# One head per stationary in the SSD layer's diagonal product: [high | low] of one head against its own decay matrix

## The chip, the cores and the metric

The kernel runs on one core of a Trainium2 chip. The metric is the device time of one execution in microseconds (us), the median of three runs before the change. The profile is of one further execution, whose span and time stand in the table below.

## The reference, cut to what matters

One layer of a decoder trunk is computed for 256 positions of width 2048: a Mamba-2 SSD mixer, then a cross-attention into 256 memory tokens, then a gated ConvFFN, each between two RMS norms, all in fp32. The change lies in the SSD mixer, in the part within a chunk (two chunks of 128 positions, 64 heads of 64 channels, 8 groups with common B and C):

```python
a = dt * (-jnp.exp(a_log))
a_cs = cumsum(a)                       # per head, along the positions of a chunk
xdt = xs * dt[..., None]
decay = exp(where(causal, a_cs[l] - a_cs[s], -inf))
cb = einsum('bclgn,bcsgn->bgcls', cm, bm)
y_diag = einsum('bgjcls,bcsgjp->bclgjp', cb[:, :, None] * decay, xdt)
...
y = y_diag + y_off + xs * d_skip
y = rmsnorm(y * silu(z), norm_g) ; return y @ w_out
```

The kernel does not carry the states from one chunk to the next separately. It treats the 256 positions as one causal product: for each head a decay matrix M of three 128x128 blocks (source chunk 0 to target chunk 0, source 0 to target 1, source 1 to target 1), and y = M applied to xdt.

## The kernel before, in words

All activations are held transposed: channels on the 128 partitions, 256 positions along the free axis. Each weight matrix comes from memory in chunks of 128x2048 fp32 (one DMA of 1 MB each on SyncE's queue) into `raw` (3 buffers), and every half chunk is split into a high part in fp32r (`hi`, ScalarE, line 139) and the remainder (`lo`, VectorE, line 153). `hi` and `lo` have 5 buffers each. An fp32 product is then made of fp32r products: `mm3` (lines 242 to 244) adds high*high, high*low and low*high; `mm2` (lines 248 and 249) does the same with a moving operand of 512 columns [high | low] for the high weights and one of 256 for the low weights.

The work is a list of slots, one for each block of 128 output channels. A slot of the SSD projections has 16 x 3 matmuls of 256 columns (line 242 to 244, `pj<-H`). The slots go by group of heads: C, B, and then four times x and z, where one x block (index i, 32 of them) holds two heads of 64 channels. Between the matmuls of the projections hang the steps of the SSD product, as hooks of later slots. For block i they are:

- `decay` and `decay_exp` (ScalarE): the exponents of the decay matrices, four blocks at a time.
- `mk_m(i)`: decay times cb on VectorE (line 515), then its high and low parts `Mh` (ScalarE, line 262) and `Ml` (VectorE, line 264), 128x768 each, one buffer each. The columns are ordered by block, then head, then target position: (a=3, h=2, l=128).
- `xs_tr(i)` and `xdt(i)`: x transposed by TensorE, multiplied by dt on VectorE into the tile `xd` (line 542, one buffer), and its high and low parts in `xdr` (ScalarE line 262, VectorE line 264).
- `y_mm(i)`: six matmuls into one PSUM bank `py` (one buffer). The stationary holds both heads' 64 channels, so each head's M is multiplied with both heads' channels: 512 columns for source chunk 0 (three matmuls), 256 for source chunk 1 (three matmuls). On rows 0 to 63 the columns of head 0 are used, on rows 64 to 127 those of head 1.
- `y_post(i)`: on VectorE, for each head, x times d_skip plus y (line 576), then times silu(z) (line 578), then the high and low parts into `G` (ScalarE line 266, VectorE line 268), the square (ScalarE line 581) and its sum (VectorE line 290).

`G` holds 16 blocks; after blocks 0 to 15 the first half of the output projection runs (16 slots with `mm2`), and after blocks 16 to 31 the second half. The order of each engine's instructions is not written out for this part: the Tile framework's scheduler merges the steps in an order of its own by a simulated time line. Each engine then takes its instructions in that order, and waits for semaphores where data or buffers are not ready.

Of the kernel before, what the change touches and what calls it, by code (L numbers as in the profile page):

```python
# [7 lines left out]
F32 = mybir.dt.float32  # L8
FR = mybir.dt.float32r
I32 = mybir.dt.int32  # L10
AF = mybir.ActivationFunctionType
OP = mybir.AluOpType

T = 256
# [13 lines left out]
PV = {}  # L28
# [33 lines left out]
def hybrid_layer_kernel(ctx, tc, xT, memT, pvd, alog, w_dt, w_in, w_kv, w_q, w_out, w_o, w_up, w_dn, out):  # L62
    nc = tc.nc
    V, S, P, PE = nc.vector, nc.scalar, nc.gpsimd, nc.tensor
# [8 lines left out]
    pv = consts.tile([128, PVN], F32, name="pv")  # L73
# [12 lines left out]
    def col(name, j):  # L86
        return pv[:, PV[name] + j:PV[name] + j + 1]
# [4 lines left out]
    B = {}  # L92
# [127 lines left out]
    def new_chunk(src, n, kind="w"):  # L220
        chunks.append((src, n, kind))
        return len(chunks) - 1
# [18 lines left out]
    def mm3(ps, whi, wlo, xhi, xlo, start, stop):  # L241
        PE.matmul(ps, whi, xhi, start=start, stop=False)  # L242
        PE.matmul(ps, whi, xlo, start=False, stop=False)  # L243
        B["mm"] = PE.matmul(ps, wlo, xhi, start=False, stop=stop)  # L244
# [13 lines left out]
    def hilo(dst, src, scale=None):  # L258

        hi, lo = dst  # L260
        if scale is None:
            S.activation(hi, src, AF.Copy)  # L262
            yield
            return V.tensor_tensor(lo, src, hi.bitcast(F32), op=OP.subtract)  # L264
        else:
            S.activation(hi, src, AF.Copy, scale=scale)
            yield
            return V.scalar_tensor_tensor(lo, src, scale, hi.bitcast(F32), op0=OP.mult, op1=OP.subtract)
# [5 lines left out]
    def halves(t):  # L274
        return t[:, 0:T], t[:, T:2 * T]
# [71 lines left out]
    wA = phA.enter_context(tc.tile_pool(name="wA", bufs=1))  # L347
# [190 lines left out]
    def xdt(i):  # L538
        def fn():
            ps = B.pop(("pt", i))  # L540
            f = wA.tile([128, T], F32, name="xd", bufs=1)
            V.tensor_tensor(f.rearrange("p (a h c) -> p a h c", a=2, h=2),
                            ps[:, :T].rearrange("p (a h c) -> p a h c", a=2, h=2),
                            dtt[:, :, 2 * i:2 * i + 2, None].to_broadcast([128, 2, 2, 64]), op=OP.mult)
            d = wA.tile([128, 2 * T], FR, name="xdr", bufs=1)
            yield from hilo(halves(d), f)
            B["xd", i] = d
        return fn

    def y_mm(i):  # L550
        def fn():
            mh, ml = B.pop(("M", i))
            d = B.pop(("xd", i))
            ps = psum.tile([128, 512], F32, name="py", bufs=1)
            mm3(ps[:, :], d[:, 0:128], d[:, 256:384], mh[:, 0:512], ml[:, 0:512], True, False)
            mm3(ps[:, 256:512], d[:, 128:256], d[:, 384:512], mh[:, 512:768], ml[:, 512:768], False, True)
            B["y", i] = ps
        return fn

# [6 lines left out]

    def y_post(i):
        def fn():
            y = B.pop(("y", i)).rearrange("p (a h l) -> p a h l", a=2, h=2)
            x = B.pop(("xsT", i)).rearrange("p (a l) -> p a l", a=2)  # L570
            sz = B.pop(("sz", i))
            t = wA.tile([128, T], F32, name="yt", bufs=1)
            t3 = t.rearrange("p (a l) -> p a l", a=2)
            for h in range(2):
                q = slice(64 * h, 64 * h + 64)
                V.scalar_tensor_tensor(t3[q], x[q], pv[q, PV["dsk"] + i:PV["dsk"] + i + 1], y[q, :, h],
                                       op0=OP.mult, op1=OP.add)
            V.tensor_tensor(t, t, sz, op=OP.mult)
            yield from hilo(halves(G[:, i % GS]), t, col("ng", i))
            sq = wA.tile([128, T], F32, name="sqy", bufs=2)  # L580
            S.activation(sq, t, AF.Square)
            yield
            ssd_norm.add(sq)
        return fn
# [44 lines left out]
    for kind, i in order:  # L629
# [13 lines left out]
        elif kind == "x":  # L643
            lane(s, w_in[blk_no], 2048, movH, xs_post(i))
            blk_no += 1
            d = 2 if i < 2 else 0
# [252 lines left out]
    for j in range(KD):  # L899
        if j % 4 == 0:  # L900
            c = new_chunk(w_o[j // 4], 2048)
# [155 lines left out]
    for i, s in enumerate(slots):  # L1057
# [29 lines left out]
        for k in range(nk):  # L1087
            for ln, ps in zip(lanes, pss):
# [4 lines left out]
                c, off, mov = ln[0], ln[1], ln[2]  # L1093
# [4 lines left out]
                x = mov[k]  # L1098
# [123 lines left out]
```

## Time and profile before

| | |
|---|---|
| median of 3 runs | 1561.46 us (1561.24 to 1563.09) |
| the profiled execution's own time | 1564.64 us |
| its span, first to last instruction | 1562.8 us |
| mean granted TensorE clock | 0.996 of 2.4 GHz |
| busy share of the span | PE 99%, weight loads 91%, DVE 77%, ACT 62%, POOL 1% |
| matmuls, weight loads | 10316, 10316 |

PE is TensorE, PEld its weight loads, DVE VectorE, ACT ScalarE, POOL GpSimd, SP SyncE. Busy times are the union of an engine's instructions. Matmuls are pipelined, so that a matmul's duration is longer than the interval to the next one's start; it is the interval that the engine's time is made of. The same holds to a smaller degree for DVE and ACT. Lines are those of the kernel before.

### The profile page before, as it was taken

The page shows a single profiled execution, that of the slowest core. Times are in us where ns is not written, and L with a number is a line of the kernel's source. Part 1 is how long each engine was busy: PE and PEld are TensorE (multiplying, and loading weights), DVE is VectorE, ACT ScalarE, POOL GpSimd, SP SyncE. Part 2 cuts the span into 40 slices and gives each one's busy share as a digit, 9 for nine tenths or more (in the row PEclk, how much of TensorE's full clock was granted, in tenths as well). Part 3 has the DMA queues.
Part 4 walks back from the last instruction along what each step waited for, and adds up shares of the span by engine and source line. Part 5 has one row for each costly group of instructions (what it writes and reads, how often), then busy time and mean ns, then how long its engine had stood idle before and what let it go on. Part 6 is the DMA issues. An engine that isn't in the chain of part 4 may idle for free. (4 is left out here: it accounts for less than half of the span.)

```text
span 1562.8 us, 25940 instructions
## 1 busy us (share of the span) xinstructions
PE 1540.4 (99%) x10316; PEld 1415.5 (91%) x10316; DVE 1202.6 (77%) x1917; ACT 966.0 (62%) x1576; POOL 10.4 (1%) x16
## 2 busy tenths in 40 slices
PE   8999999999999999999989999999999999999998
PEld 7999999889999999888989888888888888888886
DVE  7799989655898987969777887655877766778774
ACT  6698887644777774856565655544555533555563
POOL 0000000000000000000000000000000000000000
PEclk9999999999999999999989999999999999999999
DMA  7665555555555554855444555555555555555462
GB/s 268 219 217 189 174 201 189 195 189 188 160 201 178 178 170 143 314 190 169 156 137 153 196 189 187 179 200 189 189 192 188 183 198 188 192 191 193 155 212 78
DMA packets 47289, 292.10 MB, mean 187 GB/s; under 512 B 5504, under 2 KB 5568, under 8 KB 19776
## 3 DMA queue, kind: packets, MB, share of 16 engines
q1 hardware_dynamic: 46448, 289.34, 54.1%
q8 instruction: 81, 1.33, 0.4%
q10 hardware_dynamic: 720, 1.11, 0.2%
q14 instruction: 40, 0.33, 0.1%
HBM read 288.26 MB, written 2.16 MB: 186 GB/s over the span
## 5 line engine op out<-in xcount | busy, mean ns | idle before, releaser
L139 ACT ACTIVATE hi<-raw 128x1024 fp32r<-128x1024 f32 (+2 forms) x518 | 539.9, 1045 | 485.9 <-PE pj L248 386.0
L153 DVE TENSOR_TENSOR lo<-raw,hi 128x1024 fp32r<-128x1024 f32 (+2 forms) x518 | 624.1, 1207 | 262.4 <-ACT hi L139 258.0
L248 PE MATMUL pj<-H,hi 128*128 128x512 f32 x1472 | 511.8, 392 | 1.1 <-DVE ev L910 1.1
L248 PE MATMUL pj<-G,hi 128*128 128x512 f32 x1202 | 417.1, 392 | 0.0
L249 PE MATMUL pj<-H,lo 128*128 128x256 f32 x1472 | 411.6, 280 | 0.0
L242 PE MATMUL pj<-H,hi 128*128 128x256 f32 x1280 | 361.5, 283 | 6.7 <-ACT hi L262 6.3
L244 PE MATMUL pj<-H,lo 128*128 128x256 f32 x1280 | 360.2, 282 | 0.8 <-DVE lo L264 0.7
L243 PE MATMUL pj<-H,hi 128*128 128x256 f32 x1280 | 360.3, 282 | 0.0
L249 PE MATMUL pj<-G,lo 128*128 128x256 f32 x1202 | 335.4, 280 | 0.0
L248 PEld LDWEIGHTS pj<-H,hi 128*128 128x128 f32 x1472 | 276.4, 188 | 61.6 <-ACT hi L139 1.3
L249 PEld LDWEIGHTS pj<-H,lo 128*128 128x128 f32 x1472 | 276.4, 188 | 0.0
L248 PEld LDWEIGHTS pj<-G,hi 128*128 128x128 f32 x1202 | 225.3, 188 | 49.2
L242 PEld LDWEIGHTS pj<-H,hi 128*128 128x128 f32 x1280 | 241.5, 189 | 8.9 <-ACT hi L262 7.5
L244 PEld LDWEIGHTS pj<-H,lo 128*128 128x128 f32 x1280 | 241.9, 189 | 2.1 <-DVE lo L264 1.6
L243 PEld LDWEIGHTS pj<-H,hi 128*128 128x128 f32 x1280 | 242.0, 189 | 1.0
L249 PEld LDWEIGHTS pj<-G,lo 128*128 128x128 f32 x1202 | 225.7, 188 | 0.4
L920 DVE SCALAR_TENSOR_TENSOR fu<-ev,pv,fu 128x255 f32<-128x255 f32 (+1 forms) x176 | 84.2, 480 | 2.8
L456 DVE SCALAR_TENSOR_TENSOR u<-ev,pv,u 128x255 f32<-128x255 f32 (+2 forms) x144 | 68.5, 478 | 5.1 <-ACT u L452 3.9
L916 ACT ACTIVATE fu<-ev,pv 128x256 f32<-128x256 f32 x88 | 51.7, 589 | 1.4 <-DVE ev L913 0.9
L367 DVE TENSOR_TENSOR ev<-pj,rx 128x256 f32<-128x256 f32 x80 | 33.6, 421 | 13.2 <-PE pj L244 10.4
L255 DVE TENSOR_TENSOR ev<-pj,ev 128x256 f32<-128x256 f32 x92 | 38.4, 417 | 0.0
L262 ACT ACTIVATE Mh<-dec 128x768 fp32r<-128x768 f32 x32 | 26.9, 841 | 16.4 <-PE py L244 15.6
(270 smaller groups left out, 1400.8 us busy)
## 6 DMA issues: line engine op xcount, KB each, us to landing
raw<-in_w_up_dram SPq DMA_DIRECT2D x88, 1024.0 KB, 4.8
raw<-in_w_in_dram SPq DMA_DIRECT2D x78, 1024.0 KB, 4.9
raw<-in_w_out_dram SPq DMA_DIRECT2D x32, 1024.0 KB, 4.9
raw<-in_w_dn_dram SPq DMA_DIRECT2D x32, 960.0 KB, 4.6
raw<-in_w_dn_dram SPq DMA_DIRECT2D x16, 896.0 KB, 4.5
rows<-rows_d SPq DMA_DIRECT2D x32, 256.0 KB, 3.7
raw<-in_w_kv_dram SPq DMA_DIRECT2D x8, 1024.0 KB, 4.8
raw<-in_w_q_dram SPq DMA_DIRECT2D x4, 1024.0 KB, 4.8
```

The source lines that it names most:

```text
L139: S.activation(hi_t[c, h][:, :b - a], raw_t[c][:, a:b], AF.Copy)
L153: V.tensor_tensor(lo_t[c, h][:, :b - a], raw_t[c][:, a:b], hi_t[c, h][:, :b - a].bitcast(F32), op=OP.subtract)
L242: PE.matmul(ps, whi, xhi, start=start, stop=False)
L243: PE.matmul(ps, whi, xlo, start=False, stop=False)
L244: B["mm"] = PE.matmul(ps, wlo, xhi, start=False, stop=stop)
L248: PE.matmul(ps, whi, x, start=start, stop=False)
L249: B["mm"] = PE.matmul(ps[:, T:], wlo, x[:, 0:T], start=False, stop=stop)
L255: V.tensor_tensor(t, ps[:, :T], t, op=OP.add)
L367: V.tensor_tensor(t, ps[:, :T], x_norm.rbc, op=OP.mult)
L456: V.scalar_tensor_tensor(u[:, d:], ps[:, :T - d], pv[:, w + j:w + j + 1], u[:, d:], op0=OP.mult, op1=OP.add)
L916: S.activation(u, t, AF.Identity, bias=col("fb", blk), scale=pv[:, w + 2:w + 3])
L920: V.scalar_tensor_tensor(u[:, d:], t[:, :T - d], pv[:, w + j:w + j + 1], u[:, d:], op0=OP.mult, op1=OP.add)
```

## The change

In `xdt`, the high and low parts of the two heads are laid out as [high 0 | low 0 | low 1 | high 1] for each source chunk, in a tile of 128 x 768 with gaps. In `y_mm`, each head has a stationary of its own, its 64 high and its 64 low channels; the moving operand is that head's part of `Mh`, then of `Ml`: 256 columns for source chunk 0 (two pieces of 128), 128 columns for source chunk 1. That is eight matmuls, four of 256 and four of 128 columns. The result of head 0 has its high part on rows 0 to 63 and its low part on rows 64 to 127; for head 1 it is the other way round. In `y_post`, two ScalarE copies bring the low rows to the other 64 partitions, into a tile `u` that takes the buffer of `xd`, and VectorE adds them.

```diff
@@ xdt
-            d = wA.tile([128, 2 * T], FR, name="xdr", bufs=1)
-            yield from hilo(halves(d), f)
-            B["xd", i] = d
+            d = wA.tile([128, 2, 2, 192], FR, name="xdr", bufs=1)
+            flat = d.rearrange("p a h x -> p a (h x)")
+            lo = flat[:, :, 64:192].rearrange("p a (h c) -> p a h c", h=2)
+            yield from hilo((d[:, :, :, 0:64], lo), f.rearrange("p (a h c) -> p a h c", a=2, h=2))
+            B["xd", i] = flat
@@ y_mm
-            mm3(ps[:, :], d[:, 0:128], d[:, 256:384], mh[:, 0:512], ml[:, 0:512], True, False)
-            mm3(ps[:, 256:512], d[:, 128:256], d[:, 384:512], mh[:, 512:768], ml[:, 512:768], False, True)
+            m4 = [x.rearrange("p (a h l) -> p a h l", a=3, h=2) for x in (mh, ml)]
+            for h in range(2):
+                o = ps[:, h * T:(h + 1) * T]
+                for k, x in enumerate(m4):
+                    PE.matmul(o.rearrange("p (a l) -> p a l", a=2), d[:, 0, 128 * h:128 * h + 128], x[:, 0:2, h],
+                              start=k == 0, stop=False)
+                for k, x in enumerate(m4):
+                    PE.matmul(o[:, 128:], d[:, 1, 128 * h:128 * h + 128], x[:, 2, h], start=False, stop=k == 1)
@@ y_post
-            y = B.pop(("y", i)).rearrange("p (a h l) -> p a h l", a=2, h=2)
-            x = B.pop(("xsT", i)).rearrange("p (a l) -> p a l", a=2)
+            y = B.pop(("y", i)).rearrange("p (h l) -> p h l", h=2)
+            x = B.pop(("xsT", i))
             sz = B.pop(("sz", i))
+            u = wA.tile([128, T], F32, name="xd", bufs=1)
+            S.activation(u[0:64], y[64:128, 0], AF.Copy)
+            S.activation(u[64:128], y[0:64, 1], AF.Copy)
             t = wA.tile([128, T], F32, name="yt", bufs=1)
-            t3 = t.rearrange("p (a l) -> p a l", a=2)
             for h in range(2):
                 q = slice(64 * h, 64 * h + 64)
-                V.scalar_tensor_tensor(t3[q], x[q], pv[q, PV["dsk"] + i:PV["dsk"] + i + 1], y[q, :, h],
+                V.scalar_tensor_tensor(t[q], x[q], pv[q, PV["dsk"] + i:PV["dsk"] + i + 1], y[q, h],
                                        op0=OP.mult, op1=OP.add)
+            V.tensor_tensor(t, t, u, op=OP.add)
             V.tensor_tensor(t, t, sz, op=OP.mult)
```

## Rows read from the trace of the kernel before

**Rows 1.** The page: busy time by engine, and the 40 slices in tenths.
```profile
PE 1540.4 (99%) x10316; PEld 1415.5 (91%) x10316; DVE 1202.6 (77%) x1917; ACT 966.0 (62%) x1576; POOL 10.4 (1%) x16
PE   8999999999999999999989999999999999999998
```
**Rows 2.** Windows of both SSD halves: stretch, its length, busy us (instructions) by engine.
```profile
80.00:283.00 203.00, 203.00 (x1669) 200.57 (x1668) 183.97 (x305) 170.35 (x302) 0.00 (x0) 1.00 0.56 191
365.00:610.00 245.00, 245.00 (x2015) 241.98 (x2014) 207.95 (x333) 172.11 (x290) 0.00 (x0) 1.00 0.53 179
```
**Rows 3.** Waits, 80 to 283 us: engine, line, releaser: total us, times, longest.
```profile
ACT hi L139 <- PE pj L243: 17.1, 21, 2.3
ACT Mh L262 <- PE py L244: 5.3, 5, 1.5
...
DVE lo L153 <- ACT hi L139: 2.2, 6, 0.5
```
**Rows 4.** Waits, 365 to 610 us.
```profile
ACT hi L139 <- PE pj L243: 42.9, 38, 2.1
DVE lo L153 <- ACT hi L139: 22.6, 30, 3.4
...
ACT hi L139 <- PE pj L248: 6.5, 4, 1.7
```
**Rows 5.** Groups by line and shape on PE: busy us, mean ns of one.
```profile
L242 PE MATMUL py<-Mh,xdr 128*128 128x512 f32 x32 | 12.6, 394 | 0.0
...
L242 PE MATMUL py<-Mh,xdr 128*128 128x256 f32 x32 | 9.0, 280 | 0.0
```
**Rows 6.** Time line of PE, a y product: start us, duration us, instruction.
```profile
193.75 0.39 PE L244 MATMUL py<-Mh,xdr 128*128 128x512 f32 x1
193.98 0.28 PE L242 MATMUL py<-Mh,xdr 128*128 128x256 f32 x1
194.10 0.28 PE L243 MATMUL py<-Ml,xdr 128*128 128x256 f32 x1
194.21 0.28 PE L244 MATMUL py<-Mh,xdr 128*128 128x256 f32 x1
194.33 0.28 PE L243 MATMUL pj<-H,hi 128*128 128x256 f32 x1
```
**Rows 7.** Time line of PE, cb product with three matmuls of 128 columns.
```profile
62.26 0.22 PE L242 MATMUL ms<-CT,BT 128*128 128x128 f32 x1
62.32 0.28 PE L243 MATMUL ms<-CT,BT 128*128 128x128 f32 x1
62.43 0.27 PE L244 MATMUL ms<-CT,BT 128*128 128x128 f32 x1
62.54 0.33 PE L243 MATMUL pj<-H,hi 128*128 128x256 f32 x1
62.72 0.28 PE L244 MATMUL pj<-H,lo 128*128 128x256 f32 x1
```
**Rows 8.** Time line of the weight loads in the same place.
```profile
62.27 0.19 PEld L243 LDWEIGHTS ms<-CT,BT 128*128 128x128 f32 x1
62.37 0.19 PEld L244 LDWEIGHTS ms<-CT,BT 128*128 128x128 f32 x1
62.48 0.19 PEld L243 LDWEIGHTS pj<-H,hi 128*128 128x128 f32 x1
```
**Rows 9.** Time line of DVE, a y_post and the next block's xd.
```profile
195.37 0.97 DVE L576 SCALAR_TENSOR_TENSOR yt<-xsT,pv,py 64x256 f32<-64x256 f32 x2
...
198.12 0.42 DVE L578 TENSOR_TENSOR yt<-yt,sz 128x256 f32<-128x256 f32 x1
198.46 1.22 DVE L153 TENSOR_TENSOR lo<-raw,hi 128x1024 fp32r<-128x1024 f32 x1
...
200.04 0.41 DVE L542 TENSOR_TENSOR xd<-pt,dtt 128x256 f32<-128x256 f32 x1
```
**Rows 10.** Time line of ACT, a copy out of PSUM and the instruction behind it.
```profile
291.41 0.37 ACT L607 ACTIVATE m<-pj 128x256 f32<-128x256 f32 x1
291.67 1.05 ACT L139 ACTIVATE hi<-raw 128x1024 fp32r<-128x1024 f32 x1
```
**Rows 11.** Time line of DVE, the last block's G.
```profile
618.75 0.48 DVE L268 SCALAR_TENSOR_TENSOR G<-yt,pv,G 128x256 fp32r<-128x256 f32 x1 [0.58 <-ACT G L266]
```
**Rows 12.** Time line of PE, second output projection behind it.
```profile
622.66 0.62 PE L248 MATMUL pj<-G,hi 128*128 128x512 f32 x2
```

## The prediction, made before the result was known

> **What bounds the kernel now.** I read the page first, then the windows of the stage that the change touches, then who waits there, and last the time lines around single instructions. The page has TensorE (PE) busy 99% of the span, with only the first, one midway and the last of the 40 slices below nine tenths [rows 1]. The SSD product lies in two stretches, blocks 0 to 15 at about 80 to 283 us and blocks 16 to 31 at about 365 to 610 us. In both PE is busy for every microsecond: 203.00 of 203.00 and 245.00 of 245.00 [rows 2]. So in this stage the time is the number of PE's instructions times their intervals, and an interval taken from PE is time won, unless another engine comes to pace it. The nearest is VectorE (DVE): 183.97 of 203.00 busy in the first half (idle 19.0 us), 207.95 of 245.00 in the second (idle 37.1 us). ScalarE (ACT) idles for 32.7 and 72.9 us [rows 2]. What ACT waits for is mostly a free buffer for the next split (hi waits for pj: 17.1 us in 21 waits in the first half, 42.9 and 6.5 us in the second) [rows 3, 4]. A split that waits for a buffer is as far ahead as it can be, so this is time that ACT can give away. The first half has less than half of it.
>
> **PE, the term that decides.** A matmul's duration (394 ns for 512 columns, 280 ns for 256) [rows 5] is not what it takes of PE, since the next one starts earlier. The intervals: the 512-column y matmul starts at 193.75 and the next at 193.98, so 0.23 us; the three of 256 columns run from 193.98 to 194.33, so 0.117 us each [rows 6]. A block before takes 3 x 0.23 + 3 x 0.117 = 1.04 us of PE.
>
> After, a block takes eight matmuls, four of 256 and four of 128 columns. Columns fall by a third, from 2304 to 1536. But the page counts as many weight loads as matmuls [rows 1], so two matmuls with the same stationary still load it twice, and the eight have eight loads. What a 128-column fp32r matmul takes is seen in the cb product: three of them start at 62.26, the projection's matmul behind them at 62.54 and the one behind that at 62.72 [rows 7]. From 62.26 to 62.72 there are three of 128 and one of 256 columns: (0.46 - 0.117) / 3 = 0.114 us each. The weight loads there start 0.10 and 0.11 us apart [rows 8]: at 128 columns the load of the next weights sets the interval, not the columns. A 128-column matmul thus takes nearly what a 256-column one does. New block: 4 x 0.117 + 4 x 0.114 = 0.92 us. Gain 0.12 us, over 32 blocks 3.8 us.
>
> The bounds: one interval in that place is 0.06 us (62.26 to 62.32) [rows 7]. At 0.06 for all four, a block is 0.71 us and the gain 10.6 us. I take 0.114, because the short interval is repaid behind it (0.18 us from 62.54 to 62.72). On the other side, the 256-column operand is now two pieces of 128 with a gap, which no row shows. At worst it costs two intervals of 128 columns, 0.228 us, which is 0.44 us a block or 14.2 us more, a loss of 10.4 us in all; at best 0.105 us, the interval of the loads [rows 8], 1.5 us more gain. I take 0.117, the contiguous row of the same number of elements.
>
> The Trainium skill, in "TensorE: Matmul & The Clock Gate", section "Back-to-back issue gap", gives about 81 ns for each matmul of 128 columns in a sustained stream of loads and matmuls. By that figure a block would be 4 x 0.117 + 4 x 0.081 = 0.79 us and the gain 8.0 us, by estimate. The trace here has 114 ns in its own such stream, so it speaks against that figure.
>
> **DVE and ACT, the terms that should be hidden.** For each block y_post gains one DVE add of 128x256 in SBUF. Its nearest row is the multiplication on the line behind it: 0.42 us long, the next instruction 0.34 us after its start [rows 9]. 32 x 0.34 = 10.9 us on DVE, 5.4 us in each half. The two scalar_tensor_tensors keep 64x256 and read contiguous instead of strided columns; I take 0 for that: the two take 0.97 us now [rows 9], at best they would take two of the add's intervals, 0.68 us (0.3 us a block less on DVE), and nothing in their shape has grown. The high and low parts of xdr keep their element counts and get gaps, also 0. ACT gains two copies of 64x256 out of PSUM; the row is a copy of 128x256 out of PSUM, with the next instruction 0.26 us after its start [rows 10]. That is 0.52 us a block, 16.6 us in all, 8.3 us in each half. The other partition half as the target is not seen before; between 0.26 and twice that for each copy I take 0.26, since the columns set it. The cover is the idle time in rows 2: 5.4 us into 19.0 on DVE, 8.3 us into 32.7 on ACT in the first half. If the cover were gone, the 5.4 us would reach PE there.
>
> **New waits.** The copies wait at the head of ACT's queue for the last y matmul, and behind them stand the splits and Mh of the next block. ACT waits for that same event already, for Mh: 5 times, 5.3 us in the first half [rows 3]. The add waits for the copies. The tile u shares xd's one buffer, so the next block's xd multiplication (L542) waits for the add, with splits queued behind it on DVE. In the trace L576 starts at 195.37, the next L542 at 200.04 [rows 9]: 4.7 us, in which 0.97 us of L576 and the add fit. u itself waits for xd's last reader, which comes ahead of the y matmuls anyway. No DMA is added or moved on SP's queue. At the end of the stage the last block's G is written by 618.75 + 0.48 us [rows 11] and first read at 622.66 us [rows 12] (before that stand 45 matmuls of three output blocks that read the other 15): 3.4 us, against at most 0.52 + 0.34 us and the hand-over in between. All at 0.
>
> **The sum.** The profiled execution is 1564.64 us, its span 1562.8 us. 1564.64 - 3.8 = 1560.8 us. The runs' median lies 3.2 us below that execution, so the forecast for the median is 1561.46 - 3.8 = 1557.7 us. About 0.2%, 3.1 us, can be told from no change: below 1558.3 us is faster, above 1564.6 us slower. The forecast is just beyond that edge.
>
> **Rivals.**
> 1. DVE takes the first half. It is busy 91% there, and the scheduler merges everything anew. For: ACT and DVE hand splits to each other in that half with little waiting for buffers. Against: 19.0 us are idle, and PE did not wait once. If half of the added 5.4 us reaches PE, 1557.7 + 2.7 = 1560.4 us; if all, 1563.1 us. No change.
> 2. The copies block ACT's queue (the slower side). If each copy pair waits like Mh does, 5.3 / 5 = 1.06 us, a block costs ACT 1.06 + 0.52 = 1.58 us, in the first half 16 x 1.58 = 25.3 us, against 17.1 us of waits for buffers that can give way. 8.2 us then reach PE: 1557.7 + 8.2 = 1565.9 us. It decides from a wait of 17.1 / 16 - 0.52 = 0.55 us a block on. In the second half 25.3 us stay below 42.9 + 6.5 us. Against: the list of waits has 5 such waits for 16 blocks, so the scheduler mostly places what follows y late enough. The gapped operand at its upper bound (1561.46 + 10.4 = 1571.9 us) goes with this side.
> 3. The weight loads don't pace the 128-column matmuls: 1561.46 - 10.6 = 1550.9 us. For: the one short interval. Against: the sum of four intervals behind it.
> 4. The change does nothing, because PE would not be the bound: excluded by rows 2.
>
> **How the numbers follow.** Forecast 0.52, within 1556 to 1560 us, of which 0.36 lies below 1558.3 us and 0.16 above. Rival 1: 0.21, nearly all of it no change. Rival 2 with the gapped operand: 0.15. Rival 3: 0.12. Faster 0.36 + 0.12 = 0.48; same 0.16 + 0.20 = 0.36; slower 0.01 + 0.15 = 0.16. The range takes in the forecast, rival 1 and the nearer parts of 2 and 3: 1552.5 to 1565 us.
>
> **What would show it.** In the changed kernel's time line, a y matmul of 128 columns takes 0.11 us to the next start in the mean (right) or 0.06 (rival 3); a block's eight matmuls take 0.92 us together. The page counts 10316 + 64 matmuls and as many loads. PE stays busy in every microsecond of the SSD halves; idle time with DVE lo L153 or ACT hi L139 as the releaser means rival 1 or 2, and the waits of the copies for py tell which. DVE's busy time there grows by about 32 x 0.42 us, ACT's by 64 x 0.37. The forecast is wrong if the gapped operand's interval is above 0.13 us, or if PE idles for more than 1 us between 40 and 610 us.

## The result: 1578.9 us, slower

The changed kernel takes 1578.86 us (median of 4 runs, 1578.39 to 1580.44) against 1562.07 us of the kernel before in the same series, a ratio of 1.0106 with a 95% interval of 1.0095 to 1.0118. That is 16.8 us slower, where 3.8 us faster was forecast. The profiled execution took 1580.44 us, its span is 1578.7 us, 15.9 us more than before.

The page of the changed kernel, its busy times, the 40 slices of PE and the granted clock:

```profile
PE 1545.5 (98%) x10380; PEld 1422.5 (90%) x10380; DVE 1214.0 (77%) x1949; ACT 992.2 (63%) x1640; POOL 10.4 (1%) x16
PE   8999999799999999999989999999999999999998
...
PEclk9999999899999999999999999999999999999999
```

There is one new hole in PE, in the eighth slice, where before every slice but three was full [rows 1], and the clock falls in the same slice. The windows of the changed kernel around it (stretch, length, busy us and instructions of PE, PEld, DVE, ACT and POOL, granted clock, DMA share, GB/s):

```profile
100.00:280.00 180.00, 180.00 (x1509) 179.55 (x1508) 162.16 (x272) 149.27 (x270) 0.00 (x0) 1.00 0.54 183
280.00:300.00 20.00, 18.15 (x112) 16.05 (x110) 14.15 (x25) 11.17 (x24) 0.00 (x0) 1.00 0.46 163
300.00:320.00 20.00, 10.29 (x35) 8.13 (x36) 12.98 (x25) 17.27 (x34) 0.00 (x0) 0.66 0.11 25
320.00:340.00 20.00, 20.00 (x107) 17.47 (x107) 11.23 (x13) 9.19 (x13) 0.00 (x0) 0.91 0.70 238
400.00:640.00 240.00, 240.00 (x1993) 237.99 (x1992) 205.17 (x338) 179.52 (x313) 0.00 (x0) 1.00 0.53 176
```

Inside the SSD stretches PE is as full as before [rows 2]: 180.00 of 180.00 and 240.00 of 240.00 us. The loss lies between the first half and the second, in the first output projection. PE's time line there:

```profile
297.87 0.27 PE L565 MATMUL py<-Ml,xdr 128*128 128x128 f32 x1
303.08 0.80 PE L248 MATMUL pj<-G,hi 128*128 128x512 f32 x1 [4.93 <-DVE G L268]
303.68 0.41 PE L249 MATMUL pj<-G,lo 128*128 128x256 f32 x1
303.89 0.63 PE L248 MATMUL pj<-G,hi 128*128 128x512 f32 x1
304.31 0.41 PE L249 MATMUL pj<-G,lo 128*128 128x256 f32 x1
...
307.80 0.36 PE L562 MATMUL py<-Mh,xdr 128*128 128x256 f32 x1 [1.79 <-DVE xdr L264]
```

The output projection waits for the G of block 14 (4.93 us), then block 15's product waits for its `xdr` (1.79 us), and so on: 11.56 us of marked waits between 280 and 340 us (4.93, 1.79, 0.82, 3.14 and 0.88). After the first of them the interval of a 512-column matmul is 0.42 us (303.89 to 304.31) instead of 0.23 [rows 6]: the granted clock has dropped to its lower level, 1.2 GHz. It stands there from 303.1 to 306.5 us and again from 309.9 to 323.5 us. The longer intervals add 7.2 us (each interval from 270 to 345 us less its mean at the upper level and less the marked waits). 11.6 + 7.2 = 18.8 us lost. Against that stands what the product gains, below.

### The profile page after: what moved, and what is told of

The parts are those of the page before. It is cut to its first block, busy times and chain, and to the rows that moved or that the text cites. A ratio compares the mean times of both kernels' runs of the same rounds, so it can differ in the third digit from the quotient of the medians.

```text
span 1578.7 us, 26223 instructions
## 1 busy us (share of the span) xinstructions
PE 1545.5 (98%) x10380; PEld 1422.5 (90%) x10380; DVE 1214.0 (77%) x1949; ACT 992.2 (63%) x1640; POOL 10.4 (1%) x16
## 5 line engine op out<-in xcount | busy, mean ns | idle before, releaser
L248 PE MATMUL pj<-G,hi 128*128 128x512 f32 x1202 | 422.5, 395 | 9.6 <-DVE G L268 8.3
L264 DVE TENSOR_TENSOR Ml<-dec,Mh 128x768 fp32r<-128x768 f32 x32 | 30.6, 955 | 11.3 <-ACT Mh L262 10.6
```

Of the source, the lines that this page charges most:

```text
L248: PE.matmul(ps, whi, x, start=start, stop=False)
```

## Why block 15 is late: the start's lag, and a loop that can't make it up

Counted in the time lines, block 0's product starts at 86 us in both kernels, after 12.3 slots of the projections (their matmuls counted, 48 to a slot). The hooks ask for it after 6. The stage thus begins six slots late, and before the change the blocks made that up: block 12 starts 1.3 slots behind its hook (36.4 against 35.1), block 15 at 278.3 us. In the changed kernel block 12 is still 6.4 slots behind (41.5), at 268.5 us, and block 15 comes at 307.8 us. Blocks 0 to 13 stand 15.2 us apart, (284.1 - 86.0) / 13; before it was 12.8 us. No run starts the stage earlier, so the part of the lag is read from the time lines alone.

What lies in 15.2 us is a loop, since `u` lives in the one buffer of `xd`. From block 9 to 10: block 9's product starts on PE at 221.13 us (its rows stand further down); then ACT's copies and its `xdr` step, in the first fence, and DVE's steps, in the second:

```profile
222.97 0.38 ACT L583 ACTIVATE xd<-py 64x256 f32<-64x256 f32 x1
...
230.42 0.40 ACT L262 ACTIVATE xdr<-xd 128x256 fp32r<-128x256 f32 x1
```
```profile
224.72 0.97 DVE L588 SCALAR_TENSOR_TENSOR yt<-xsT,pv,py 64x256 f32<-64x256 f32 x2
...
227.26 0.42 DVE L590 TENSOR_TENSOR yt<-yt,xd 128x256 f32<-128x256 f32 x1
...
228.44 0.43 DVE L542 TENSOR_TENSOR xd<-pt,dtt 128x256 f32<-128x256 f32 x1
...
232.83 0.42 DVE L264 TENSOR_TENSOR xdr<-xd,xdr 128x256 fp32r<-128x256 f32 x1
```

The next product follows at 236.39 us. The instructions of the loop are short; between them stand splits and decays, about 1 to 3 us at each hand-over. Nothing in it shows as a long wait, and neither ACT nor DVE is full (149.27 and 162.16 of 180.00 us between 100 and 280 us). The shared buffer can act as a wait on the chip and through the order that the scheduler gives the queues; no run separates the two.

PE does not feel the lag while it has projections, and for a while behind them: with four PSUM buffers `pj` (read from the code) it runs ahead in four output blocks with every G that is ready. At 297.9 us it has done 56 pairs of `mm2` (four blocks times 14 G's, 19.4 us at 0.347 us a pair), and then nothing is left.

On ACT a long step then stands ahead of block 15's `xdr`, whose `xd` DVE has written by 302.16 us:

```profile
302.83 1.28 ACT L508 ACT_TABLE_LOAD   x1
304.12 2.76 ACT L508 ACTIVATE dec<-dec 128x3072 f32<-128x3072 f32 x1
306.79 0.40 ACT L262 ACTIVATE xdr<-xd 128x256 fp32r<-128x256 f32 x1
```

This is the exponential of the next four decay matrices. By the code it overwrites the tile that block 15's M is made from, so it comes behind block 14's product and is late with it; in the kernel before it starts at 273.57 us. By these rows some 4 us of block 15's lateness are this step, an estimate: no run moves it alone.

## The experiments

The first four take the change apart. **Own buffer:** `u` in the buffer of a tile used once at the start.

```diff
-            u = wA.tile([128, T], F32, name="xd", bufs=1)
+            u = wA.tile([128, T], F32, name="rowt", bufs=1)
```

> The changed kernel, but u takes a buffer of its own (that of a tile used once at the start) instead of the one buffer of xd. Theory A (the shared buffer ties the next block's xd to this block's add, so that the 32 blocks become one serial loop, 15.2 us a block, which can't make up the start's lag before the output projection): the loop opens, the y products of blocks 12 to 15 come back to about 240 to 280 us, PE no longer idles at 298 to 318 us, and the time is the kernel before less 3.8 us, 1557 to 1560 us. Theory B (the added work on ACT and DVE is what makes y late): still 1572 to 1579 us. Theory C (every y matmul now needs the low part of xdr, so the product as such starts later): still 1572 to 1579 us.

1562.61 us against 1562.30 (ratio 1.0002, 0.9993 to 1.0011). Block 15 starts at 282.9 us, and the hole is gone. The shared buffer is thus necessary for the loss. But the expected 3.8 us of gain are not there: the time is that of the kernel before. The window of the hole in this kernel:

```profile
280.00:340.00 60.00, 60.00 (x353) 52.99 (x352) 38.81 (x51) 34.04 (x54) 0.00 (x0) 1.00 0.54 188
```

**The wait alone:** the kernel before, with y_post's first step written into `xd`.

```diff
-            t3 = t.rearrange("p (a l) -> p a l", a=2)
+            w = wA.tile([128, T], F32, name="xd", bufs=1)
+            t3 = w.rearrange("p (a l) -> p a l", a=2)
...
-            V.tensor_tensor(t, t, sz, op=OP.mult)
+            V.tensor_tensor(t, w, sz, op=OP.mult)
```

> The kernel before, with nothing added or moved but a buffer: the two scalar_tensor_tensors of y_post write into the one buffer of xd, and the multiplication by silu(z) reads it there. Theory A: the same loop arises without the copies and the add, blocks of the first half 14 to 15 us apart instead of 12.8, PE idle behind 282 us, 1570 to 1580 us. Theories B and C: as before, 1561 to 1563 us.

1563.76 us, ratio 1.0011 (1.0002 to 1.0020). The loop arises as expected, blocks 0 to 14 stand 14.2 us apart and block 15 starts at 295.3 us, 17 us later than before. But the time hardly moves; I had expected 8 us at least. The 17 us are taken up by the four open output blocks, and PE idles for 1.6 us, at the upper clock throughout:

```profile
280.00:340.00 60.00, 58.41 (x340) 51.24 (x339) 39.67 (x57) 36.28 (x58) 0.00 (x0) 1.00 0.57 196
```

So lag is free up to an edge, and this kernel stands on it.

**The product alone:** the changed kernel without the copies and the add, its low rows left out.

```diff
-            u = wA.tile([128, T], F32, name="xd", bufs=1)
-            S.activation(u[0:64], y[64:128, 0], AF.Copy)
-            S.activation(u[64:128], y[0:64, 1], AF.Copy)
...
-            V.tensor_tensor(t, t, u, op=OP.add)
```

> The changed kernel without the two copies and the add (the low rows are left out of the result). Theory A: no wait on xd, 3.8 us under the kernel before, 1557 to 1559 us. Theory B: the same. Theory C: 1572 to 1579 us. If a y product of 0.92 us were wrong, the time would show it here: 1551 us at 0.06 us for 128 columns.

1560.21 us, ratio 0.9988 (0.9979 to 0.9996): 2.1 us faster, less than the 3.8. Block 15 is at 277.8 us, so the new product as such delays nothing.

**The work alone:** the kernel before with copies and add into a buffer of their own, the result unused.

```diff
+            u = wA.tile([128, T], F32, name="rowt", bufs=1)
+            u3 = u.rearrange("p (a l) -> p a l", a=2)
+            S.activation(u3[0:64], y[64:128, :, 0], AF.Copy)
+            S.activation(u3[64:128], y[0:64, :, 1], AF.Copy)
...
+            V.tensor_tensor(u, t, u, op=OP.add)
```

> The kernel before with the copies and the add as extra work, in a buffer of their own; their result is used by nothing. Theory A: hidden, 1561 to 1564 us. Theory B: 1574 to 1582 us.

1563.70 us, ratio 1.0012 (1.0003 to 1.0021): 1.4 us, nearly hidden; block 15 at 284.4 us.

No part alone costs more than 1.5 us. What is left is their combination, and the next run makes it without the new product. **Wait and work:** the kernel of the work alone, with its tile in `xd`.

```diff
-            u = wA.tile([128, T], F32, name="rowt", bufs=1)
+            u = wA.tile([128, T], F32, name="xd", bufs=1)
```

> The kernel before, its product untouched, with the two copies and the add as extra work whose result is used by nothing, and their tile in the one buffer of xd. Theory A2 (the wait on xd and the copies inside that wait together stretch the loop to some 15 us a block; the start's lag is then not made up, and the first output projection runs out of products whose G is ready; each alone stays under that edge): block 15's product behind 303 us, 1574 to 1581 us. Theory D (it takes the new product, each of whose matmuls needs both parts of xdr, to stretch the loop): 1563 to 1567 us.

1576.99 us against 1562.32, ratio 1.0092 (1.0079 to 1.0106). One name in the kernel that took 1563.70 us brings 13.3 us. Block 15 starts at 299.6 us, 3 us earlier than expected, and PE has the hole in the same place, with 7.6 us of marked waits and 2.8 us by the lower clock:

```profile
280.00:340.00 60.00, 52.38 (x293) 45.07 (x292) 39.60 (x60) 38.53 (x69) 0.00 (x0) 0.94 0.44 154
```

Two runs shorten the loop but leave the shared buffer. **Early release:** `u` is read by the first VectorE step instead of the third.

```diff
-            for h in range(2):
-                q = slice(64 * h, 64 * h + 64)
-                V.scalar_tensor_tensor(t[q], x[q], pv[q, PV["dsk"] + i:PV["dsk"] + i + 1], y[q, h],
-                                       op0=OP.mult, op1=OP.add)
-            V.tensor_tensor(t, t, u, op=OP.add)
+            V.scalar_tensor_tensor(t, x, col("dsk", i), u, op0=OP.mult, op1=OP.add)
+            for h in range(2):
+                q = slice(64 * h, 64 * h + 64)
+                V.tensor_tensor(t[q], t[q], y[q, h], op=OP.add)
```

> The changed kernel with u still in xd's buffer, but y_post's steps in another order: x times d_skip plus u first, in one instruction over all 128 partitions, then the two additions of y out of PSUM (three VectorE instructions as before). u is free after the first instead of after the third. Theory A2: the loop loses about 2 us (212.81 to 214.95 us in the trace of the changed kernel), 14 us a block or less, block 15's product at 290 to 298 us, PE waits little, 1559 to 1565 us. Theory E (the copies' own place in ACT's queue makes the lag, whatever is released when): 1572 us or more.

1573.11 us, ratio 1.0063 (1.0051 to 1.0076). The lag behaves as expected, block 15 at 296.4 us, but the time doesn't: 8 us above the range. With block 15 only 1.1 us later than in the wait alone, PE idles for 6.4 us and the clock falls with it:

```profile
280.00:340.00 60.00, 53.62 (x288) 46.57 (x287) 37.41 (x57) 37.53 (x65) 0.00 (x0) 0.89 0.43 154
```

The longest wait there is not for G but 3.9 us for `BT`, which the second half's first group needs. ACT writes it at 302.33 us, and ahead of that ACT works without a pause from 291.3 us on: six decay steps, the same exponential (294.46 to 298.53 us with its table load), splits, block 15's copies and a second table load. In the wait alone the last step of BT's convolution stands ahead of the exponential (291.04 against 292.72 us). Blocks 13 and 14 are also 4.9 and 4.4 us later than there. The edge is thus sharper than block 15's lag: what the engines have queued at that point decides.

**High priority:** the scheduler is told to put the loop's steps first.

```diff
-                hook(s + 2, "late", xdt(i))
-                hook(s + 3, "pe", y_mm(i), 6)
-                hook(s + 3, "late", y_post(i))
+                hook(s + 2, "late", hot(xdt(i)))
+                hook(s + 3, "pe", hot(y_mm(i)), 6)
+                hook(s + 3, "late", hot(y_post(i)))
```

> The changed kernel with the steps xdt, y_mm and y_post of blocks 2 to 30 marked as high priority for the scheduler; the shared buffer stays. Theory A2: the loop's steps no longer stand behind splits, the lag is made up, no idle PE at 298 to 318 us, 1558 to 1563 us. Theory F (the engines' total work in the first half is the limit, so that what goes first costs the splits): PE waits for hi or lo, 1566 us or more.

1571.24 us, ratio 1.0056 (1.0042 to 1.0070): neither side. The lag stays, block 15 at 298.3 us, PE busy 52.77 of the 60 us, and neither hi nor lo is what it waits for there. Why priority shortens the loop so little is open.

**Own buffer and early release together**, the version that the runs point to:

> The changed kernel with u in a buffer of its own and the order of the early release. If the last block's chain is what costs the own-buffer kernel its gain: 1560 to 1561 us; if the work as such, as with the own buffer alone: 1562 to 1563 us.

1560.62 us, ratio 0.9989 (0.9980 to 0.9998): faster than both kernels, by 1.7 and 18 us. Block 15 is at 279.3 us and the hole is gone:

```profile
280.00:340.00 60.00, 60.00 (x351) 52.91 (x350) 37.63 (x51) 36.07 (x54) 0.00 (x0) 1.00 0.56 197
```

It does without two waits of 0.8 us that the own buffer alone has at 627 and 645 us, in the second output projection; that accounts for most of the 2.0 us between the two medians, though their intervals overlap. The two waits are for an output block's `m` and for a split, not for the last block's G, so the reason that the expectation gives is not shown.

Two runs on that version. **The 128-column matmuls twice:**

```diff
-                for k, x in enumerate(m4):
+                for k, x in enumerate(m4 + m4):
-                    PE.matmul(o[:, 128:], d[:, 1, 128 * h:128 * h + 128], x[:, 2, h], start=False, stop=k == 1)
+                    PE.matmul(o[:, 128:], d[:, 1, 128 * h:128 * h + 128], x[:, 2, h], start=False, stop=k == 3)
```

> The own-buffer, early-release kernel (1560.6 us) with each matmul of 128 columns issued twice (source chunk 1 is counted twice in the result): 128 more matmuls of 128 columns. If the weight loads set their interval, 0.11 us each: 14.1 us more, 1573 to 1576 us. If their columns did, 0.06 us each: 7.7 us more, 1567 to 1569 us.

1574.77 us, 14.15 us more: 14.15 / 128 = 0.111 us for each. The two runs stand in different series; each against the kernel before in its own, it is 12.25 + 1.70 = 13.95 us, 0.109 us each. The columns are not what they cost.

**The sum of squares on GpSimd:**

```diff
-                return V.tensor_tensor(self.accs[0], self.accs[0], sq, op=OP.add)
+                return (eng or V).tensor_tensor(self.accs[0], self.accs[0], sq, op=OP.add)
...
-            ssd_norm.add(sq)
+            ssd_norm.add(sq, eng=P)
```

> The own-buffer, early-release kernel with the running sum of squares (one 128x256 add a block, line 290, needed only at the stage's end) on GpSimd instead of VectorE, so that VectorE has as many instructions a block as in the kernel before. If VectorE's added work still costs PE something: 1559 to 1560 us. If the two engines hinder each other or PE is the only bound: 1560.5 us or more.

1563.27 us, ratio 1.0004 (0.9995 to 1.0013), 2.7 us more than without it (2.5 us, each against the kernel before in its own series). The two engines hinder each other: GpSimd takes 1031 ns for what takes VectorE 418 ns, and the scalar_tensor_tensor into G, 480 ns in the kernel before, takes 629 ns here. The 19 of them that overlap a GpSimd add take 735 ns in the mean, the other 13 take 474 ns. (Groups by line of this kernel: busy us, mean ns of one.)

```profile
L290 POOL TENSOR_TENSOR sqy<-sqy 128x256 f32<-128x256 f32 x31 | 32.0, 1031 | 563.5 <-ACT sqy L593 563.5
```
```profile
L268 DVE SCALAR_TENSOR_TENSOR G<-yt,pv,G 128x256 fp32r<-128x256 f32 x32 | 20.1, 629 | 10.8 <-ACT G L266 10.8
```

The Trainium skill, in "SBUF — State Buffer", section "Who interferes with whom", says that a VectorE instruction with two inputs in SBUF contends with a GpSimd instruction that reads SBUF, because its second input comes through a read interface that the two share. The trace agrees with it: the scalar_tensor_tensor into G has two such inputs, `yt` and `G`, and is the one that grows, 735 against 474 ns.

## The prediction, step by step

**PE's term was right.** A block's product in the changed kernel:

```profile
221.13 0.28 PE L562 MATMUL py<-Mh,xdr 128*128 128x256 f32 x1
221.25 0.28 PE L562 MATMUL py<-Ml,xdr 128*128 128x256 f32 x1
221.37 0.22 PE L565 MATMUL py<-Mh,xdr 128*128 128x128 f32 x1
221.43 0.28 PE L565 MATMUL py<-Ml,xdr 128*128 128x128 f32 x1
221.54 0.33 PE L562 MATMUL py<-Mh,xdr 128*128 128x256 f32 x1
221.71 0.28 PE L562 MATMUL py<-Ml,xdr 128*128 128x256 f32 x1
221.83 0.23 PE L565 MATMUL py<-Mh,xdr 128*128 128x128 f32 x1
221.89 0.27 PE L565 MATMUL py<-Ml,xdr 128*128 128x128 f32 x1
222.00 0.33 PE L242 MATMUL pj<-H,hi 128*128 128x256 f32 x1
222.17 0.28 PE L243 MATMUL pj<-H,hi 128*128 128x256 f32 x1
```

From 221.13 to 222.17 there are the eight and one of the projection: 1.04 - 0.117 = 0.92 us, as forecast. The short interval behind a 128-column matmul (0.06) is repaid two matmuls later (0.17), as in rows 7. The gapped operand costs nothing: 221.25 to 221.37 is 0.12 us. So rival 3 is out, and the doubled matmuls give the same 0.111 us from the other side. The figure of about 81 ns that the Trainium skill gives in "TensorE: Matmul & The Clock Gate", section "Back-to-back issue gap", does not hold for this stream, which takes 111 ns; the measurement decides.

Over the whole stage in the kernel with the product alone, the y matmuls' intervals sum to 27.7 us instead of 33.6, and the projections behind them are 1.6 us longer: a gain of 4.3 us. The run shows 2.1 us. PE waits 0.5 us for `BT` there, in an interval 0.66 us too long, and some 3200 projection intervals are 118.4 instead of 118.0 ns in the mean, 1.5 us; where the latter comes from is open.

**"New waits ... All at 0" is the step that failed.** I named the wait of L542 for the add and measured its slack at one place, 4.7 us between L576 and the next L542 [rows 9]. Two things were wrong in that. The slack belonged to a kernel in which nothing tied the two: the changed one has the copies ahead of L588, the add 2.5 us behind it (224.72 to 227.26), and L542 behind that. And a slack at one block says nothing about a loop over 16 blocks that starts six slots late and has to run faster than the projections to be in time at the end. I did not look for the lag, nor for what needs its end. What the runs showed in place of the 0: with that wait and the copies inside it one turn takes 15.2 us instead of 12.8, PE stands for 11.6 us behind the stage's first half, and the lower clock adds 7.2 us. Without the shared buffer (own buffer) neither is there.

**The cover held, but the cover was not the question.** DVE and ACT have no more to do than I said (DVE 1214.0 busy against 1202.6 us, forecast 32 x 0.42 = 13; ACT 992.2 against 966.0, forecast 64 x 0.37 = 24), and the work alone costs 1.4 us. Rival 1 was that work taking the first half, and rival 2 the copies blocking ACT ahead of the splits. PE waits for neither hi nor lo in the hole, and the copies wait for `py` once in the whole kernel, 3.6 us: it is neither of the two. Rival 2 had the sign right, and the loss does need the copies (the wait alone costs 1.5 us), but as a part of the loop and not because they hold up the splits.

**The last sentence of the prediction was the right test**: PE idling by more than 1 us between 40 and 610 us. It idles 11.6 us there.

**The sum after the fact:** 11.6 + 7.2 us lost, 4.3 us gained, 14.5 us; the spans of the two profiles differ by 15.9 us. The rest, 1.4 us, is of the size of what the product alone lost of its gain, 2.2 us.

## What to carry to other kernels

A tile that takes the name of another with one buffer adds an edge between two steps; ask whether it closes a loop over the iterations, how long one turn is with the queues as they stand, and whether that loop has a lag to make up. Look at how far the loop is behind its due place over the whole stage, not at the slack of one turn: here 17 us of lag at the last block cost under 2 us in one kernel, 18 us cost 12 in another, and 30 us cost 19. A product with fewer columns is worth only the intervals that it saves; where each matmul loads its own weights, 128 columns cost 0.11 us and 256 cost 0.117.

## What was not expected of the hardware

An idle PE can cost more than its idle time: in the changed kernel 11.6 us of waits between 298 and 318 us brought the granted clock to the lower level, which cost another 7.2 us, and in the early-release kernel 6.4 us brought 5.8. In the wait alone 1.6 us of waits left the clock at its upper level. A copy from PSUM into the other 64 partitions (L583, 64x256) takes 381 ns, the 128x256 copy that stays on its partitions 364 ns in the mean.
